# Mixer of a hybrid encoder: head sums by transpose and VectorE, and probabilities scaled before they are transposed, on one Trainium2 core

## Chip, core and metric

One core of a Trainium2 chip runs the whole program. The metric is the device time of one execution in microseconds (us); lower is better. Before the change it is 826.89 us, the median of 3 runs (826.85 to 827.06).

## What is computed

One layer of an encoder on 512 positions of width 1024, all in float32. Three stages follow each other:

```python
x = x + 0.5 * swiglu(rms_norm(x, ffn1_norm), ffn1_w_gate, ffn1_w_up, ffn1_w_down)
h = rms_norm(x, mix_norm)
u = h @ w_in                       # [ fourier 512 | q 8x64 | k 2x64 | v 2x64 ]
f_out = fourier_mixer(u[..., :o0], fnet_w, fnet_b)
a_out = gqa_attention(u[..., o0:o1], u[..., o1:o2], u[..., o2:], q_norm, k_norm)
x = x + jnp.concatenate([f_out, a_out], axis=-1) @ w_out
x = x + 0.5 * swiglu(rms_norm(x, ffn2_norm), ffn2_w_gate, ffn2_w_up, ffn2_w_down)
return rms_norm(x, final_norm)
```

The change touches the middle stage, and in it the attention:

```python
q = rms_norm(q.reshape(b, s, N_Q_HEADS, HEAD_DIM), q_norm)     # per head of 64
k = rms_norm(k.reshape(b, s, N_KV_HEADS, HEAD_DIM), k_norm)
q, k = apply_axial_rope(q, tables), apply_axial_rope(k, tables)
scores = jnp.einsum('bqhgd,bkhd->bhgqk', q_blk, k) * scale
p = jax.nn.softmax(scores, axis=-1)
return jnp.einsum('bhgqk,bkhd->bqhgd', p, v)
```

An `rms_norm` divides by the root of the mean square plus 1e-6. Since `q` and `k` come from `h`, whose own norm factor `r` (one number for each position) can be left out of the product and put in later, the kernel works on unnormed projections and corrects with `r` where it must.

## The kernel before

**Layout.** Activations lie transposed: the model width on the 128 partitions, the 512 positions along the free axis. A 128x512 float32 tile fills one of the eight PSUM banks. Every float32 factor is split into a high part in the format fp32r and the rest, so a product is two or three matmuls on TensorE (PE); ScalarE (ACT) rounds off the high part, VectorE (DVE) subtracts to get the rest (the helper `lows`, L127). Each weight chunk costs a 512 KB load on SP's queue (`raw_...`), a cast on ACT and a subtraction on DVE.

**Mixer.** The stage stands between the two FFNs. It is cut into named steps (`k.0`, `s001`, `e001` and so on), and a table `ORDER` lists all of them; the engines' queues are filled in exactly this order, each engine taking its own instructions from it. Nothing is reordered on the chip: an engine that reaches an instruction whose input isn't there waits, and everything listed behind it on that engine waits too. The eight banks are handed out in the order of the table as well: a step that takes a bank waits until the step that last reads the bank's former content is through.

The steps that matter here, with `t` the head pair 0 to 3, `b` the head of the pair, `c` a block of 128 queries and `kc` a block of 128 keys:

- `k.0` to `k.7`, `q0.0` and so on, `v.0` and so on: the projections, 3 matmuls of 512 columns each (L183). `n1.c`: the sum of squares of `x` over the partitions, 4 matmuls with a tile of ones as the moving operand, so 2 columns each (L241). `n1.m`, `n1.p`: mean, and the power -1/2 on GpSimd (POOL), which gives `r`. `n1.t`, `n1.b`: `r` transposed into a row over the free axis (4 PE transposes, L260) and copied out by ACT.
- `k.sq`, `q0.sq`: squares by ACT (L841). `.pq`: the sum of squares of each head, again 4 matmuls of 2 columns (`halves`, L889). `.s0`: three small DVE instructions that bring in `r` twice (L896, L898, L899); `.s1`: the power on POOL (L903); `.s2`: one more small DVE instruction (L907).
- `.sw`, `.rc`, `.rs`: the rotary embedding. `cos` loads its two tables on SP's queue. `.ah`, `.al`, `.bh`, `.bl`: the split of the rotated queries; `kw`, `kp`, `km`, `k0.0` and so on: the same for keys, after their factor was turned by 4 PE transposes (L946).
- `vt`, `vp`, `v0.h`, `v0.l`, `v1.h`, `v1.l`: values, scaled by the row of `r` on DVE, turned on PE and split.
- `s###`: two matmuls of 512 columns give the scores of 128 queries against all keys (L1150, L1151). `m###`: their maximum on DVE (L1156, L1157). `e###`: the exponential on ACT, with the sum `z` of each row as a by-product (L1164). `t###`: 4 PE transposes (L1176) turn a block so that keys lie on the partitions. `h###`, `l###`: the split by ACT (L1181) and DVE (L127). `v###`: two matmuls with the values (L1219).
- `z#.r`, `z#.w`, `z#.p`: 1/z by DVE (L1196), spread over 128 columns by POOL (L1201) and turned by 4 PE transposes (L1208); `o##.c`, `o##.a`: the two parts of the output added; `r#.m`: the multiplication by the turned 1/z on DVE (L1240); `r#.h`, `r#.l`: the split for the output projection.
- `f##.#`, `d##`, `c#.#`, `map#`: the Fourier group; `y#.#`: the output projection, 64 steps of 3 matmuls, of which `y#.0` to `y#.3` need the Fourier group alone.

Of the kernel before, what the change touches and what calls it, by code (L numbers as in the profile page):

```python
# [47 lines left out]
wk.r wq0.r wv.r wk.h wk.l wq0.h k.0 cos k.1 wv.h wq1.r wq0.l k.2 k.3 wv.l wq2.r k.4 k.5 k.6 k.7 k.sw k.rc k.rs  # L48
q0.0 f0.r q0.1 q0.2 q0.3 k.sq n1.c n1.m wq1.h n1.p wq1.l q0.4 q0.5 q0.6 q0.7 wq2.h q0.rc v.0 wq3.r q0.sw wq2.l
q1.0 k.pq k.s0 f2.r q0.rs q0.ah v.1 v.2 v.3 q0.sq q0.bh k.s1 k.s2 kw q0.al v.4 v.5 v.6 kp km n1.t n1.b v.7  # L50
wq3.h q0.bl pos vt wq3.l k1.2 q0.pq q1.1 q1.2 q0.s0 k1.0 k1.1 k1.3 vp q1.3 q1.4 q1.5 q1.6 q1.7 k0.0 k0.2 v0.h
k0.1 f1.r k0.3 s001 s000 q0.s1 q1.sw q0.s2 v0.l f0.h q1.sd s002 s010 m001 q1.sq q1.pq s003 q2.0 q2.1 q2.2 q2.3
m002 m010 q1.s0 e010 q2.4 q2.5 e001 q2.6 f0.l v1.h q2.7 m003 m000 e002 e003 s011 e000 t000 t001 h001 q1.rc
q1.rs v1.l q3.0 q2.sw f1.h f1.l m011 l001 h000 l000 q2.sd q2.sq t002 s012 m012 h002 fw.r l002 q1.ah q1.al
q2.rc q3.1 q3.2 q3.3 q3.4 q3.5 q3.6 q3.7 q1.bh q1.bl e012 s100 e011 s102 q2.rs q3.sw q3.rc s013 m013 t003 f2.h
q2.bh q1.s1 q1.s2 v000 v001 f00.0 f2.l v002 q3.sq m100 q2.pq e013 q3.sd m102 h003 l003 t010 q2.ah q2.al e100
t013 e102 s101 m101 e101 f00.1 q2.bl f00.u t011 h011 v003 q2.s0 s103 t012 q3.rs q3.bh l011 f02.0 m103 s110
q3.pq h010 l010 v010 v011 o00.c o00.a s201 h012 l012 s111 e103 q3.s0 t100 q3.bl h013 l013 q3.ah t102 h100 m110
v012 v013 o01.c f3.r f02.1 h102 l100 s112 q3.s1 m111 e111 o01.a t101 s113 z0.r z0.w l102 f01.0 h101 e110 m112
z0.p l101 q2.s1 v100 e112 v101 m113 e113 s203 s200 t103 r0.m r0.h f02.e h103 f02.h z1.r q3.s2 q2.s2 m200 z1.w  # L60
e200 l103 r0.l t110 h110 t112 q3.al f01.1 v102 m203 v103 o10.c m201 f01.u l110 o0.r s202 m202 h112 f03.0 o10.a
f03.1 f3.h v110 f03.e t113 e201 t111 f03.h s210 f3.l f03.l f10.0 f10.1 o1.r l112 s211 h111 l111 v111 h113 v112
e203 f10.u l113 s212 m210 m211 e202 t200 m212 t202 s300 f02.l e210 t201 h202 l202 e211 v113 m300 h200 f12.0
h201 l200 l201 f12.1 fw.h fw.l s213 m213 e212 s301 t203 o11.c z1.p v200 v201 v202 o11.a r1.m f12.e e213 t210
s303 h203 l203 e300 t211 h210 f11.0 h211 r1.h m301 l210 l211 s302 f12.h t212 v203 e301 m303 o20.c f13.0 m302
r1.l e302 f12.l s311 f11.1 h212 o20.a m311 z2.r t213 v210 f13.1 l212 s310 o0.h o0.l o3.r map0 o2.r h213 f11.u
l213 e303 t300 t302 f13.e o1.h m310 o1.l v211 v212 v213 t301 f13.h e310 f13.l d00 o21.c o21.a d10 map1 h302
z2.w l302 z2.p map0.h map0.l t303 h300 e311 s312 map1.h l300 v300 r2.m d20 h303 o2.h m312 d01 map1.l s313 d11
h301 l303 l301 v301 m313 d0.h d0.l v302 v303 c0.s e312 e313 t312 t311 o2.l d1.h d1.l o30.c c0.q c0.c d21 h312
o30.a o6.r t310 h310 l312 h311 c1.c c0.o c0.h d31 l310 t313 z3.r z3.w d2.h o4.r l311 c1.s c1.q v310 d30 d3.h  # L70
v311 h313 v312 c0.l y0.0 y1.0 d2.l c2.s r2.h c2.c c1.o l313 y2.0 v313 c1.h d3.l z3.p c2.q c3.c c2.o c2.h c1.l
c3.s c2.l y1.1 c3.q y0.1 o31.c y2.1 y2.2 c3.o c3.h c3.l y1.2 y1.3 y0.2 y0.3 y2.3 y0.4 r2.l y0.5 y0.6 o31.a
r3.m r3.h r3.l y0.7 o3.h o3.l y2.4 y2.5 y2.6 y1.4 y1.5 y1.6 y1.7 y1.x o4.h y3.0 o5.r y3.1 o4.l y3.2 y3.3 y3.4
y3.5 y2.7 o5.h y3.6 y3.7 o6.h y2.x o7.r y0.x o6.l y0.q y4.0 y4.1 y4.2 y4.3 y4.4 o5.l y4.5 y4.6 y4.7 y2.q y1.q
y4.x y3.x y5.0 y5.1 y5.2 y3.h o7.h y1.h o7.l y1.l y1.a y2.a y5.3 y6.0 y0.h y5.4 y0.l y3.q y3.a y4.h y5.5 y5.6
y5.7 y5.x y6.1 y6.2 y6.3 y6.4 y6.5 y6.6 y4.q y5.q y4.a y5.h y6.7 y6.x y6.h y7.0 y7.1 y7.2 y7.3 y6.q y4.l y2.h
y7.4 y7.5 y7.6 y7.7 y5.l y3.l y2.l y5.a y6.a y6.l y7.x y7.q y7.h y7.l y7.a
# [8 lines left out]
def encoder(ctx, tc, A, out):  # L86
# [660 lines left out]
    with tc.tile_pool(name="mix", bufs=1) as mp, tc.tile_pool(name="mixt", bufs=1) as mt:  # L747
# [9 lines left out]
        room(mp, 32)  # L757
# [122 lines left out]
        def heads_ops(name, t, factor):  # L880

            v = sc[:, :, 2 * t : 2 * t + 2]
            rx = n1.r.unsqueeze(2).to_broadcast([P, 4, 2])

            @op(f"{name}.pq")
            def _():
                banks[f"pq{name}"] = pq = bank_for(f"pq{name}")
                for c in range(4):
                    nc.tensor.matmul(  # L889
                        pq[:, 2 * c : 2 * c + 2], sqs[name][:, c * P : (c + 1) * P], halves, start=True, stop=True  # L890
                    )

            @op(f"{name}.s0")
            def _():
                pq = banks[f"pq{name}"][:, 0:8].rearrange("p (c t) -> p c t", t=2)
                nc.vector.tensor_tensor(out=v, in0=pq, in1=rx, op=ALU.mult)  # L896
                read(f"pq{name}")
                nc.vector.tensor_tensor(out=v, in0=v, in1=rx, op=ALU.mult)  # L898
                nc.vector.tensor_scalar(out=v, in0=v, scalar1=1.0 / HD, scalar2=EPS, op0=ALU.mult, op1=ALU.add)  # L899

            @op(f"{name}.s1")
            def _():
                nc.gpsimd.tensor_tensor(out=v, in0=v, in1=mhalf.rearrange("p (c t) -> p c t", t=2), op=ALU.pow)  # L903

            @op(f"{name}.s2")
            def _():
                nc.vector.scalar_tensor_tensor(out=v, in0=v, scalar=factor, in1=rx, op0=ALU.mult, op1=ALU.mult)  # L907
# [55 lines left out]
        @op("vt")  # L963
        def _():
            rots["v"] = tp.tile([P, S], F32, tag="g", name="vt")
            nc.vector.tensor_tensor(out=rots["v"], in0=banks["v"], in1=n1.rb, op=ALU.mult)
            read("v")

        @op("vp")
        def _():  # L970
            banks["vp"] = vp = bank_for("vp", 2)
# [3 lines left out]
        def value_ops(v):  # L975


            def own():
                return banks["vp"].rearrange("p (c v e) -> p c v e", c=4, v=2)[:, :, v, :]

            op(f"v{v}.h")(lambda: nc.scalar.copy(vst[:, v, :, 0, :], own()))

            @op(f"v{v}.l")
            def _():
                lows(vst[:, v, :, 1, :], own(), vst[:, v, :, 0, :])
                read("vp")

        for v in range(2):
            value_ops(v)

# [200 lines left out]
        def sum_ops(t):  # L1191


            @op(f"z{t}.r")
            def _():
                nc.vector.reciprocal(zs[t], zs[t])  # L1196

            @op(f"z{t}.w")
            def _():
# [367 lines left out]
```

## Time and profile before

| | us |
|---|---|
| median of 3 runs | 826.89 |
| the profiled execution | 827.06 |
| its span from first to last instruction | 824.8 |
| first FFN, from the start to | 331.06 |
| mixer, from there to | 489.87 |
| second FFN and final norm, from there to the end | 824.8 |

The stage borders are starts of matmuls on PE: the mixer's first one, and the first `gu` product of the second FFN. The profile counts an engine as busy from the start to the end of its instructions, and these overlap: on ACT and DVE an instruction often starts about 0.1 us before its forerunner's end, and on PE several matmuls are in flight at once. So two measures of an instruction's cost are needed, its duration and the distance to the next start. A wait is listed with the engine that waited, what it waited for, the total, the number of times and the longest.

### The profile page before, as it was taken

The page shows a single profiled execution, that of the slowest core. Times are in us where ns is not written, and L with a number is a line of the kernel's source. Part 1 is how long each engine was busy: PE and PEld are TensorE (multiplying, and loading weights), DVE is VectorE, ACT ScalarE, POOL GpSimd, SP SyncE. Part 2 cuts the span into 40 slices and gives each one's busy share as a digit, 9 for nine tenths or more (in the row PEclk, how much of TensorE's full clock was granted, in tenths as well). Part 3 has the DMA queues.
Part 4 walks back from the last instruction along what each step waited for, and adds up shares of the span by engine and source line. Part 5 has one row for each costly group of instructions (what it writes and reads, how often), then busy time and mean ns, then how long its engine had stood idle before and what let it go on. Part 6 is the DMA issues. An engine that isn't in the chain of part 4 may idle for free.

```text
span 824.8 us, 13679 instructions
## 1 busy us (share of the span) xinstructions
PE 816.9 (99%) x5406; PEld 750.4 (91%) x5406; DVE 639.2 (78%) x1005; ACT 464.6 (56%) x778; POOL 30.7 (4%) x34
## 2 busy tenths in 40 slices
PE   9999999999999999999999999999999999999997
PEld 7889999899989998888999888899988999899986
DVE  7998896489756947699998488998955896479574
ACT  7764664167524645677786357556632674256462
POOL 0110000000000000221100000100000000000001
PEclk9999999999999999999999999999999999999999
DMA  7664322323242213522020224453232332422222
GB/s 256 180 145 173 122 91 77 122 103 141 78 140 102 64 55 115 184 93 77 26 77 27 82 97 116 119 163 123 90 122 94 128 116 63 138 103 97 69 77 103
DMA packets 31168, 89.58 MB, mean 109 GB/s; under 512 B 3712, under 2 KB 8832, under 8 KB 31104
## 3 DMA queue, kind: packets, MB, share of 16 engines
q1 hardware_dynamic: 27776, 82.61, 29.2%
q0 software_dynamic: 2608, 5.12, 3.4%
q8 instruction: 42, 0.69, 0.3%
q10 hardware_dynamic: 720, 0.98, 0.3%
q14 instruction: 22, 0.18, 0.1%
HBM read 84.24 MB, written 2.10 MB: 105 GB/s over the span
## 4 chain that ended last, share of the span: by engine, by line
PE 92%; DVE 5%; issue 1%; ACT 0%; DMA 0%; POOLq 0%; POOL 0%; DVEq 0%; ACTq 0%
PE dn L183 25%; PE r L419 23%; PE q L419 12%; PE gu L183 8%; PE mix L183 7%; PE p L419 6%; PE gu L708 3%; PE mix L1219 1%; PE mix L1176 1%; DVE mx L1156 1%; PE mix L1073 1%; DVE pl L127 1%; PE mix L1015 1%; PE mix L1016 1%; PE mix L1014 1%
## 5 line engine op out<-in xcount | busy, mean ns | idle before, releaser
L419 PE MATMUL r<-rt,ring 128*128 128x256 f32 x1686 | 209.2, 276 | 0.0
L183 PE MATMUL dn<-at,ring 128*128 128x512 f32 x900 | 203.3, 381 | 0.5 <-DVE ring L127 0.4
L419 PEld LDWEIGHTS r<-rt,ring 128*128 128x128 f32 x1686 | 200.3, 188 | 0.8
L183 PEld LDWEIGHTS dn<-at,ring 128*128 128x128 f32 x900 | 168.0, 188 | 29.8 <-DVE ring L127 1.6
L419 PE MATMUL q<-rt,ring 128*128 128x256 f32 x840 | 106.6, 276 | 0.0
L127 DVE TENSOR_TENSOR ring<-s,ring 128x1024 fp32r<-128x1024 f32 x70 | 85.4, 1220 | 24.1 <-ACT ring L378 20.8
L419 PEld LDWEIGHTS q<-rt,ring 128*128 128x128 f32 x840 | 100.4, 188 | 0.0
L543 DVE SCALAR_TENSOR_TENSOR gx<-dn,gx 128x512 f32<-128x512 f32 x61 | 41.9, 688 | 67.6 <-PE dn L183 67.6
L378 ACT CAST ring<-s 128x1024 fp32r<-128x1024 f32 x70 | 73.5, 1050 | 28.0 <-PE p L419 13.7
L169 ACT CAST ring<-raw_dn 128x768 fp32r<-128x768 f32 (+3 forms) x58 | 45.2, 783 | 71.3 <-PE dn L183 62.1
L127 DVE TENSOR_TENSOR ring<-raw_dn,ring 128x768 fp32r<-128x768 f32 (+3 forms) x58 | 51.5, 891 | 5.6 <-PE r L419 4.4
L419 PE MATMUL p<-rt,ring 128*128 128x256 f32 x420 | 53.3, 276 | 0.0
L127 DVE TENSOR_TENSOR ring<-raw_g,ring 128x1024 fp32r<-128x1024 f32 x35 | 42.7, 1219 | 11.1 <-PE p L419 10.2
L419 PEld LDWEIGHTS p<-rt,ring 128*128 128x128 f32 x420 | 50.2, 188 | 0.0
L183 PE MATMUL gu<-ring 128*128 128x512 f32 x216 | 48.9, 381 | 0.0
L183 PEld LDWEIGHTS gu<-ring 128*128 128x128 f32 x216 | 40.4, 188 | 6.9
L378 ACT CAST ring<-raw_g 128x1024 fp32r<-128x1024 f32 x35 | 36.8, 1051 | 16.0 <-DMA raw_g<-in_wgu 8.8
L427 ACT COPY p<-r 128x256 f32<-128x256 f32 x35 | 12.9, 370 | 46.7 <-PE r L419 46.3
L451 ACT ACTIVATE g<-g 128x512 f32<-128x512 f32 x35 | 22.2, 633 | 23.4 <-DVE g L450 23.1
L387 ACT CAST ring<-raw_u 128x512 fp32r<-128x512 f32 x35 | 21.8, 624 | 16.6 <-PE q L419 16.0
L255 POOL TENSOR_TENSOR r<-ms,mhalf 128x4 f32<-128x4 f32 (+1 forms) x4 | 4.3, 1072 | 659.5 <-DVE ms L248 659.5
L464 DVE TENSOR_TENSOR u<-g,u 128x512 f32<-128x512 f32 x35 | 24.0, 685 | 6.1 <-ACT u L463 6.0
(271 smaller groups left out, 1323.1 us busy)
## 6 DMA issues: line engine op xcount, KB each, us to landing
raw_g<-in_wgu SPq DMA_DIRECT2D x35, 512.0 KB, 3.6
raw_u<-in_wgu SPq DMA_DIRECT2D x35, 512.0 KB, 4.3
raw_dn<-in_wd SPq DMA_DIRECT2D x40, 384.0 KB, 3.1
raw_gu<-in_wgu SPq DMA_DIRECT2D x12, 512.0 KB, 3.5
raw_o<-in_wo SPq DMA_DIRECT2D x8, 512.0 KB, 3.5
raw_dn<-in_wd SPq DMA_DIRECT2D x8, 448.0 KB, 3.4
raw_wq<-in_wins SPq DMA_DIRECT2D x4, 512.0 KB, 5.1
raw_f<-in_winf SPq DMA_DIRECT2D x4, 512.0 KB, 4.1
```

The source lines that it names most:

```text
L127: nc.vector.tensor_tensor(out=lo, in0=src, in1=asf(hi), op=ALU.subtract)
L169: nc.scalar.copy(hi[:, :n, :], raw[:, :n, :])
L183: nc.tensor.matmul(ps, a, b, start=first and b is mhi and a is whi, stop=last and a is wlo)
L378: nc.scalar.copy(hi, src)
L387: nc.scalar.copy(hi, src)
L419: nc.tensor.matmul(ps[:, t], a[:, ks], b[:, i, t], start=first and i == 0 and o == 0, stop=i == KH - 1 and o == 2, skip_group_check=not first,
L427: nc.scalar.copy(t, ps)
L451: nc.scalar.activation(b["g"], b["g"], AF.Silu)
L464: nc.vector.tensor_tensor(out=u, in0=b["g"], in1=u, op=ALU.mult)
L543: nc.vector.scalar_tensor_tensor(out=x[d][:, t], in0=ps[:, t], scalar=0.5, in1=x[d][:, t], op0=ALU.mult, op1=ALU.add)
L708: nc.tensor.matmul(turned(pss[c]), w[:, k % 2, c], turned(m[k]), start=k == 0 and m is hh and w is hi, stop=k == KD - 1 and w is lo,)
L1014: nc.tensor.matmul(ps, hh[k][:, cs], whi[:, a, :], start=k == 0, stop=False)
```

## The change

Four things, and a new `ORDER` table (633 steps before, 657 now).

1. The sums of squares (`n1.c` and the five `.pq`) no longer multiply with ones. The squares are transposed (4 PE transposes of 128 columns) and DVE adds along the free axis with one `tensor_reduce`. The small corrections with `r` are gone: instead of bringing `r` in twice, the eps is multiplied by the mean square of the position (`eps_ms`) and added to the sum. `.s2` is gone, and the factor that was in it is the key's `scalar1` in `kw`.
2. The row of `r` (`n1.t`, `n1.b`) is gone. Values are copied out by ACT, turned, and multiplied by `r` on DVE, now with positions on the partitions (`vs`); their split is one step each instead of two (`v.h`, `v.l`).
3. `z#.r`, `z#.w`, `z#.p` and `r#.m` are gone. For each pair of heads and query block DVE takes 1/z (`g##`, 128x2), and ACT multiplies each 128x512 block of probabilities by it in place (`n###`); the transposes `t###` now read these.
4. The order of everything around it.

```diff
-q0.0 f0.r q0.1 q0.2 q0.3 k.sq n1.c n1.m wq1.h n1.p wq1.l q0.4 q0.5 q0.6 q0.7 wq2.h q0.rc v.0 wq3.r q0.sw wq2.l
+wk.r wq2.r wq0.r wq1.r wk.h wk.l wv.r k.0 k.1 wq0.h k.2 wq0.l k.3 wq1.h k.4 k.5 k.6 k.7 n1.c k.sq q0.0 cos
...
-        room(mp, 32)
+        eps_ms = mp.tile([P, 8], F32, name="eps_ms")[:, :4]
...
-                    nc.tensor.matmul(
-                        pq[:, 2 * c : 2 * c + 2], sqs[name][:, c * P : (c + 1) * P], halves, start=True, stop=True
-                    )
+                    nc.tensor.transpose(pq[:, c * P : (c + 1) * P], sqs[name][:, c * P : (c + 1) * P], ident)
...
-                pq = banks[f"pq{name}"][:, 0:8].rearrange("p (c t) -> p c t", t=2)
-                nc.vector.tensor_tensor(out=v, in0=pq, in1=rx, op=ALU.mult)
+                pq = banks[f"pq{name}"].rearrange("p (c t e) -> p c t e", c=4, t=2)
+                nc.vector.tensor_reduce(out=v, in_=pq, axis=AX.X, op=ALU.add)
                 read(f"pq{name}")
-                nc.vector.tensor_tensor(out=v, in0=v, in1=rx, op=ALU.mult)
-                nc.vector.tensor_scalar(out=v, in0=v, scalar1=1.0 / HD, scalar2=EPS, op0=ALU.mult, op1=ALU.add)
+                nc.vector.tensor_tensor(out=v, in0=v, in1=er, op=ALU.add)
...
-            @op(f"{name}.s2")
-            def _():
-                nc.vector.scalar_tensor_tensor(out=v, in0=v, scalar=factor, in1=rx, op0=ALU.mult, op1=ALU.mult)
...
-                nc.vector.tensor_copy(kw, sc[:, :, 0:2].unsqueeze(3).to_broadcast([P, 4, 2, HD]))
+                nc.vector.tensor_scalar(
+                    out=kw, in0=sc[:, :, 0:2].unsqueeze(3).to_broadcast([P, 4, 2, HD]),
+                    scalar1=HD**0.5, scalar2=None, op0=ALU.mult,
+                )
...
-            nc.vector.tensor_tensor(out=rots["v"], in0=banks["v"], in1=n1.rb, op=ALU.mult)
+            nc.scalar.copy(rots["v"], banks["v"])
...
+        @op("vs")
+        def _():
+            nc.vector.tensor_tensor(
+                out=rots["v"].rearrange("p (c e) -> p c e", c=4),
+                in0=banks["vp"].rearrange("p (c e) -> p c e", c=4),
+                in1=n1.r.unsqueeze(2).to_broadcast([P, 4, P]), op=ALU.mult,
+            )
+            read("vp")
...
-        def sum_ops(t):
...
-                nc.vector.reciprocal(zs[t], zs[t])
...
-                nc.gpsimd.tensor_copy(zw, zs[t].unsqueeze(3).to_broadcast([P, 4, 2, HD]))
...
-                    nc.tensor.transpose(zps[t][:, c * P : (c + 1) * P], zs[t][:, c].rearrange("p a b -> p (a b)"), ident)
+        def sum_ops(t, c):
+            z = lambda b: zs[t][:, c, b : b + 1]
+
+            @op(f"g{t}{c}")
+            def _():
+                nc.vector.reciprocal(zs[t][:, c], zs[t][:, c])
+
+            for b in range(2):
+                op(f"n{t}{b}{c}")(lambda b=b: nc.scalar.activation(prob[t, b, c], prob[t, b, c], AF.Copy, scale=z(b)))
...
-                nc.vector.tensor_tensor(out=pair[t], in0=zps[t], in1=pair[t], op=ALU.mult)
...
-                n1.sum(banks["ss"], c, [n1.acc])
+                nc.tensor.transpose(ss[:, c * P : (c + 1) * P], n1.acc[:, c * P : (c + 1) * P], ident)
...
-            n1.mean(banks["ss"], 0, 4)
+            nc.vector.tensor_reduce(out=n1.ms, in_=banks["ss"].rearrange("p (c e) -> p c e", c=4), axis=AX.X, op=ALU.add)
             read("ss")
+            nc.vector.tensor_scalar(out=n1.ms, in0=n1.ms, scalar1=1.0 / D, scalar2=EPS, op0=ALU.mult, op1=ALU.add)
+            nc.vector.tensor_scalar(out=eps_ms, in0=n1.ms, scalar1=HD * EPS, scalar2=None, op0=ALU.mult)
```

**How the order moves instructions.** First place: PE at the start of the mixer, from the key projection (`mix0`) to the values or queries that follow. `mix` with a number is a PSUM bank. Before:

```order
L183 MATMUL mix0_3406<-ring_61 128x4x32x4 x24
L183 MATMUL mix1_3407<-ring_61 128x4x32x4 x12
L241 MATMUL mix2_3408<-ones_86,acc1_94 128x2 x4
L183 MATMUL mix1_3407<-ring_61 128x4x32x4 x12
L183 MATMUL mix3_3409<-ring_61,more_3401 128x4x32x4 x3
L183 MATMUL mix4_3410<-ring_61 128x4x32x4 x3
L889 MATMUL mix5_3411<-halves_111,sq_k_3482 128x2 x4
```

Now:

```order
L184 MATMUL mix0_3406<-ring_61 128x4x32x4 x24
L1286 MATMUL mix1_3407<-ident_106,acc1_94 128x128 x4
L184 MATMUL mix2_3408<-ring_61 128x4x32x4 x6
L890 MATMUL mix3_3409<-ident_106,sq_k_3460 128x128 x4
L184 MATMUL mix2_3408<-ring_61 128x4x32x4 x18
L184 MATMUL mix4_3410<-ring_61 128x4x32x4 x3
L943 MATMUL mix5_3411<-ident_106,kw_3414 128x128 x4
```

The sum over `x` follows the keys at once, the sum over the keys' squares 6 matmuls later instead of 30, and both are transposes of 128 columns where they were matmuls of 2.

Second place: ACT at the first probabilities, from the load of the exponential's table to the first casts of turned blocks (`ph`). `e` is a block of probabilities, `z0` their row sums. Before:

```order
L1164 ACT_TABLE_LOAD
L1164 ACTIVATE e010_3674,z0_3673<-mix7_3413,mx010_3667,sc_3405 128x512
L1164 ACTIVATE e001_3682,z0_3673<-mix5_3411,mx001_3641,sc_3405 128x512
L981 CAST near_3399<-mix2_3408 128x4x64
L1164 ACTIVATE e002_3698,z0_3673<-mix6_3412,mx002_3664,sc_3405 128x512
L1164 ACTIVATE e003_3700,z0_3673<-mix0_3406,mx003_3692,sc_3405 128x512
L1164 ACTIVATE e000_3704,z0_3673<-mix1_3407,mx000_3695,sc_3405 128x512
L1181 CAST ph001_3714<-mix5_3411 128x512
```

Now, the later part of the same piece:

```order
L1157 ACTIVATE e012_3687,z0_3637<-mix7_3413,mx012_3665,sc_3405 128x512
L912 CAST near_3399<-rot_q1_3603 64x512
L1192 ACTIVATE e002_3654<-e002_3654,z0_3637 128x512
L921 CAST near_3399<-rot_q1_3603 64x512
L1192 ACTIVATE e001_3643<-e001_3643,z0_3637 128x512
L1192 ACTIVATE e012_3687<-e012_3687,z0_3637 128x512
L1157 ACTIVATE e000_3732,z0_3637<-mix6_3412,mx000_3716,sc_3405 128x512
L1157 ACTIVATE e003_3734,z0_3637<-mix0_3406,mx003_3698,sc_3405 128x512
L963 COPY vt_3752<-mix1_3407 128x512
L1192 ACTIVATE e000_3732<-e000_3732,z0_3637 128x512
L1192 ACTIVATE e003_3734<-e003_3734,z0_3637 128x512
```

Before, the turned blocks came right after the five exponentials; now eight exponentials (of both heads, since `g##` takes a pair) and the in-place products (L1192) stand ahead of the first transposes, and the copy of the values (L963) has moved between them.

More of the change, by code (lines that the diff above doesn't have):

```diff
@@ L53 @@
[L53 to L57, printed above, removed]
@@ L1273, in output_ops @@
                 op(f"{name}.a")(lambda: nc.vector.tensor_tensor(out=n2.acc, in0=n2.acc, in1=sqs[name], op=ALU.add))
-        scale = HD**-0.5
         for c, n in enumerate(("k", "q0", "q1", "q2", "q3", "v")):
@@ L1278, in encoder @@
         rope_ops("k", qkg[:, 1:2])
-        heads_ops("k", 0, 1.0)
+        heads_ops("k", 0)
         key_ops()
@@ L1282, in encoder @@
             query_ops(t)
-            heads_ops(f"q{t}", t + 1, scale)
-            sum_ops(t)
+            heads_ops(f"q{t}", t + 1)
+            for c in range(4):
+                sum_ops(t, c)
             result_ops(t)
```

97 lines of the change are left out of this document (38 added, 59 removed).

## Prediction

> **What bounds the kernel now.** I read the page's first two parts first: is one engine full?
>
> ```profile
> span 824.8 us, 13679 instructions
> PE 816.9 (99%) x5406; PEld 750.4 (91%) x5406; DVE 639.2 (78%) x1005; ACT 464.6 (56%) x778; POOL 30.7 (4%) x34
> ```
>
> PE is busy for 99% of the span. A busy PE may still stretch its matmuls, so next I read busy time by stretches, for the mixer alone: its opening, the attention from the first score to the last weighted values, and what follows.
>
> ```profile
> core 0: us, PE busy (x) PEld busy (x) DVE busy (x) ACT busy (x) POOL busy (x), PEclk, DMA share, GB/s
> 331.06:356.11 25.05, 25.05 (x133) 21.76 (x132) 19.16 (x33) 17.39 (x25) 6.61 (x6) 1.00 0.61 205
> 356.11:448.41 92.30, 92.02 (x614) 83.55 (x613) 87.55 (x180) 71.38 (x145) 8.73 (x7) 1.00 0.16 52
> 448.41:489.87 41.46, 41.46 (x195) 35.50 (x193) 25.66 (x37) 17.31 (x26) 0.00 (x0) 1.00 0.22 77
> ```
>
> PE idles 0.28 us in the whole mixer, and its granted clock is 1.00 in each stretch. In the attention DVE is nearly full too (87.55 of 92.30) and ACT has 20.9 us free. The list of waits says how close DVE and ACT come to holding PE up:
>
> ```profile
> PEld mix L1150 <- ACT e L1164: 0.4, 1, 0.4
> PEld mix L1150 <- DVE pl L127: 0.4, 1, 0.4
> PEld mix L1176 <- ACT e L1164: 0.2, 1, 0.2
> ```
>
> Three short waits in 92 us. So PE's own work sets the end of the mixer, with two engines a step behind it, and every microsecond of PE work taken out counts in full as long as ACT and DVE stay ahead.
>
> **What leaves PE.** The chain of waits gives the price of each removed or added piece, as the time in which PE hands out its instructions:
>
> ```profile
> 331.06 7.92 PE mix L183 x36
> 338.98 0.79 PE mix L241 x8
> 343.86 0.79 PE mix L889 x8
> 349.17 0.44 PE mix L260 x4
> 393.38 0.44 PE mix L1208 x4
> ```
>
> Four matmuls of 2 columns appear as 8 records and take 0.79 us; four transposes of 128 columns take 0.44. The change replaces six such sums (`n1.c`, five `.pq`): out 6 x 0.79 = 4.74, in 6 x 0.44 = 2.64. It drops the row of `r` (L260) and four turns of 1/z (L1208): out 5 x 0.44 = 2.20. Together PE loses 4.74 + 2.20 - 2.64 = 4.30 us. All of it stands in the chain, so none was hidden.
>
> The one doubt is whether a transpose always costs 0.11.
>
> ```profile
> L1176 PE MATMUL mix<-ident,e 128*128 128x128 f32 x128 | 17.7, 272 | 0.0
> ```
>
> One lasts 272 ns from start to end, but neighbours overlap, so I take 0.11. If the new ones could not overlap, the 20 dropped and 24 added ones would go by 0.27, and PE would lose 4.74 - 4 x 0.27 = 3.65; I keep 3.65 as the lower end. A rule speaks against the change: the Trainium skill, "TensorE: Matmul & The Clock Gate", section "Part 4: PE-mode transpose", gives about 275 ns for a 128x128 transpose inside a kernel and says that transposes don't count as PE work for the full clock. The 272 ns agree with its figure; its clock effect isn't seen here, where 128 transposes ran in a mixer whose granted clock stayed 1.00. By the page's figure the sum would be the lower end, 3.65. With 4 transposes more than before in all, the clock rule gets no chance of its own.
>
> **What comes to ACT.** 32 multiplications of 128x512 by a number per partition. No row has exactly this; the nearest is the scaling by the gain (L209: from and to SBUF, 512 wide, scale per partition).
>
> ```profile
> L209 ACT ACTIVATE ring<-gx 128x512 fp32r<-128x512 f32 x9 | 6.3, 714 | 4.9 <-DVE gx L1262 4.9
> 332.77 0.72 ACT L209 ACTIVATE ring<-gx 128x512 fp32r<-128x512 f32 x1
> 333.40 0.62 ACT L219 ACTIVATE sq<-gx 128x512 f32<-128x512 f32 x1
> ```
>
> It lasts 0.714 but the next one starts 0.63 after it. So 32 cost ACT 20 us by starts, 22.8 by durations; I take 20, since ACT's queue in the attention is mostly back to back. Against the 20.9 us free that fills ACT to the brim, if the stretch stayed as it is. The new order stretches it: the first score now comes after 21.6 us of PE's work in the mixer instead of 24.8, and steps of the output projection move in before the last block, so that counted by these prices PE has 97.0 us of work between first score and last weighted values (90.3 before by the same prices, against 92.30 measured). Counted by starts in the same way, ACT has 88.6 us there and DVE 91.5.
>
> **DVE** comes out even.
>
> ```profile
> 356.90 0.68 DVE L1156 TENSOR_REDUCE mx<-mix 128x1 f32<-128x512 f32 x1
> 357.61 0.16 DVE L1157 TENSOR_TENSOR mx<-mx,sc 128x1 f32<-128x1 f32 x1
> 357.69 0.68 DVE L1156 TENSOR_REDUCE mx<-mix 128x1 f32<-128x512 f32 x1
> 395.31 0.19 DVE L1196 RECIPROCAL z<-z 128x8 f32<-128x8 f32 x1
> 395.42 0.19 DVE L907 SCALAR_TENSOR_TENSOR sc<-sc,r 128x8 f32<-128x8 f32 x2
> L1240 DVE TENSOR_TENSOR oo<-mix,oo 128x512 f32<-128x512 f32 x4 | 2.7, 687 | 0.1
> ```
>
> Six sums over 512 elements are new: by the maximum (L1156) 0.7 each, against four small instructions of 0.15 to 0.2 that go with each `.pq` and one that stays: +0.1 x 5, and +1.0 for `n1.m`. Sixteen reciprocals at 0.11 instead of four: +1.3. Four multiplications by the turned 1/z go: -2.7. The values' scaling only moves. Sum about 0. POOL loses four copies and gains nothing.
>
> **Where the new wait may come.** The transposes now need the scaled blocks, and a block can be scaled only after the exponentials of both heads and DVE's `g##`. I follow ACT from the second score of the new order (`s011`) to the first transposes (`t000`), with these starts:
>
> ```profile
> 359.44 1.28 ACT L1164 ACT_TABLE_LOAD   x1 [1.95 <-DVE sc L896]
> 360.74 0.78 ACT L1164 ACTIVATE e<-mix,mx,sc 128x512 f32<-128x512 f32 x1
> 361.50 0.77 ACT L1164 ACTIVATE e<-mix,mx,sc 128x512 f32<-128x512 f32 x1
> ...
> 366.58 0.69 ACT L849 ACTIVATE own_q<-mix,qkg 128x512 f32<-128x512 f32 x1
> 367.16 0.59 ACT L1181 CAST ph<-mix 128x512 fp32r<-128x512 f32 x1
> 367.63 0.62 ACT L841 ACTIVATE sq_q<-mix 128x512 f32<-128x512 f32 x1
> 368.12 0.61 ACT L1181 CAST ph<-mix 128x512 fp32r<-128x512 f32 x1
> 368.58 0.63 ACT L918 CAST near<-rot_q 64x512 fp32r<-64x512 f32 x1
> 369.24 0.62 ACT L927 CAST near<-rot_q 64x512 fp32r<-64x512 f32 x1
> 369.88 0.78 ACT L1164 ACTIVATE e<-mix,mx,sc 128x512 f32<-128x512 f32 x1
> ```
>
> After the score, about 1.0 for the maximum on DVE; table load 1.3; eight exponentials at 0.76 (360.74 to 361.50), 6.1; one `own` and one `sq`, 0.6 + 0.5; two query casts, 1.3; the values' copy, 0.5; five scalings at 0.63 and the last one's tail, 3.2. That is 14.5 us. PE has between the two 48 matmuls of 0.22 (36 take 7.92 in the chain), six pairs for scores at 0.44 and two groups of transposes at 0.44: 14.1 us.
>
> So PE waits some 0.4 us there, and everything listed behind `t000` with it. From there on ACT and DVE are each at 90 to 95% of PE, and the old order shows that this can be run with hardly a wait (DVE at 95%, three waits). But two engines are close now, and each `g##` on DVE waits for an exponential on ACT, with maxima queued behind it. I add 0.6 us for this, between 0 (both have room by the count above) and the rival's price below. New waits: 1.0; old waits gone: 0.28.
>
> **Sum.** The profiled execution took 827.06, of which 824.8 are the span; it lies 0.2 above the median. 827.06 - 4.30 - 0.28 + 1.0 = 823.5, and relative to the median **823.3 us**. With no wait at all it is 822.2, with transposes at their full length and waits of 1.9, 824.8: that is the forecast's own range.
>
> **Rivals.**
>
> *Faster, but the opening is late.* The load of `wv` now stands ahead of `cos` on SP's queue, and waits until DVE has read the buffer of `wq0`.
>
> ```profile
> 331.09 0.33 SPq L1300 DMA_DIRECT2D cos<-in_cos  x1
> 331.95 1.23 DVE L127 TENSOR_TENSOR ring<-raw_wq,ring 128x1024 fp32r<-128x1024 f32 x1 [0.17 <-ACT ring L812]
> raw_wv<-in_wins SPq DMA_DIRECT2D x1, 512.0 KB, 3.5
> cos<-in_cos SPq DMA_DIRECT2D x1, 256.0 KB, 2.7
> ```
>
> So `cos` goes out at 333.5 instead of 331.09 and lands between 336.2 and, if it shares the way with `wv`, 339.5; `k.rc` wants it at 338.0 (keys done at 336.3, four transposes, one reduce and two small ones). Up to 1.5 us late, with `k.rs`, `q0.rc`, the query casts and the first score behind it, which has 0.5 us of play by the same kind of count: 824.3.
>
> *About the same: the removed work was not what held the end.* If DVE's chain paces the attention, PE only trades work for waits: 826.9. For it: DVE's 95%. Against: DVE idles 4.7 us there while PE idles 0.28.
>
> *About the same, or slower: ACT and DVE hold each other up.* The sixteen `g##` stand in DVE's queue; when one waits for its exponential, the maxima behind it come late, hence the next exponentials, hence the next `g##`. DVE has 97.0 - 91.5 = 5.5 us of play; 3.6 of these were there before (90.3 - 86.7), and were needed, as the three waits show. So 1.9 us are free, and what sixteen waits take beyond that PE waits too. At 0.3 us each PE loses 2.9: 822.5 + 2.9 = 825.4. At one whole exponential each (0.77) it loses 10.4: **832.9, slower**. It decides from 0.5 us each on (8.0 - 1.9 = 6.1: 828.6). For it: ACT is near full, so an exponential is rarely early. Against: in the new table ACT's and DVE's work per 8 us of PE stays level, counted by these prices between 6.0 and 9.3 and between 6.6 and 10.5, with no stretch in which both pile up.
>
> **Chances.** Forecast 0.66, late opening 0.06, removed work not binding 0.05, mutual waits below 0.5 us each 0.12 (a quarter of it still faster), above 0.11. A measurement of this kernel tells a change of 0.2%, 1.65 us, from none. Faster by more: 0.66 + 0.06 + 0.03 = 0.75. Within: 0.09 + 0.05 = 0.14. Slower: 0.11. The range of 8 in 10 goes from 822.2 to 827.0: it leaves out the slow rival, a few hundredths of the mutual waits, and an even larger gain.
>
> **What would show it.** Right: PE's records fall by 48 (24 sums of 2 columns) and rise by 4 transposes, the mixer from first projection to first `gu` product takes 154.5 to 156 us instead of 158.8, the new scalings start 0.6 apart, ACT is busy above 85% of the attention, and PE idles at most 2 us there, the first time at `t000`. Wrong: scalings above 0.7 apart, or DVE waiting at the reciprocals for more than 0.3 us each (mutual waits); `k.rc` ended by the load of `cos` (opening); the mixer at 158 us or more with PE waiting on `pl` and `e` throughout.

## The result and the profile after

| | before | after |
|---|---|---|
| median, runs taken side by side, us | 826.97 (826.85 to 827.36, 4 runs) | 822.3 (821.47 to 822.44, 4 runs) |
| profiled execution, us | 827.06 | 822.25 |
| first FFN, to the mixer's first matmul | 330.90 | 331.46 |
| mixer, to the first `gu` product | 158.97 | 154.16 |
| the rest | 334.92 | 334.80 |

The ratio is 0.994 [0.9925, 0.9955]. On the forecast's scale that is 826.89 x 0.994 = 821.9 (820.7 to 823.2 by the interval): 1.4 below the forecast and 0.3 below the lower end of the range. The stages here begin where the first matmul starts; the chain of waits, which gave 331.06 and a mixer of 158.8, takes that matmul over a little later.

The page's first rows after the change:

```profile
span 820.4 us, 13609 instructions
PE 813.2 (99%) x5362; PEld 745.9 (91%) x5362; DVE 638.9 (78%) x1004; ACT 482.4 (59%) x809; POOL 28.1 (3%) x30
```

PE has 44 records fewer (48 of 2 columns out, 4 transposes in). Busy time by stretches, with the columns of the same view in the prediction: the mixer's opening, the attention, what follows.

```profile
331.46:353.36 21.90, 21.90 (x108) 18.50 (x107) 17.96 (x28) 16.61 (x24) 5.77 (x5) 1.00 0.52 180
353.36:451.94 98.58, 98.36 (x636) 88.61 (x635) 91.88 (x190) 91.59 (x181) 6.94 (x4) 1.00 0.18 60
451.94:485.62 33.68, 33.68 (x154) 28.72 (x153) 21.47 (x28) 15.82 (x23) 0.00 (x0) 1.00 0.24 79
```

PE fills each stretch, at a granted clock of 1.00. What changed in the attention is ACT's column: 91.59 of 98.58, where it had 71.38 of 92.30. ACT carries the new work and PE hardly sees it. The list of waits, first for PE and its weight loads, then a row of DVE's own:

```profile
PEld mix L1143 <- DVE near L128: 0.6, 1, 0.6
PE mix L1143 <- DVE near L128: 0.2, 1, 0.2
...
DVE z L1189 <- ACT e L1157: 0.9, 2, 0.7
```

One wait is left in the mixer, at a product of scores (L1143) and not at the transposes (L1169). The chain of waits over the stretch before it says what is late there; columns are start, us and the piece of work.

```profile
361.79 0.58 ACT own_q L850
362.37 0.77 ACT e L1157 x2
363.14 0.02 issue
363.16 0.17 DVE z L1189
363.32 0.60 DVE mx L1149
363.92 0.02 issue
363.95 0.16 DVE mx L1150
364.11 0.61 DVE mx L1149
...
365.74 0.70 DVE near L128
366.43 0.04 issue
366.48 0.49 PE mix L1143
```

Read it backwards. The score `s103` needs the rest of q1's split (`near`, step `q1.al`). DVE came to that late, because two maxima and a sum stand ahead of it, and ahead of these a reciprocal that waited 0.72 us for an exponential. The weights came 0.6 us late. What the stream of matmuls lost by it is read from the starts on PE:

```profile
365.42 0.84 PE L184 MATMUL mix<-ring 128*128 128x512 f32 x3
366.48 0.49 PE L1143 MATMUL mix<-ks,near 128*128 128x512 f32 x1 [0.22 <-DVE near L128]
366.80 0.39 PE L1144 MATMUL mix<-ks,near 128*128 128x512 f32 x1
```

Products of 512 columns start 0.22 apart here, so the third of the first row starts at 365.86. The next one follows 0.61 later and the one behind it 0.33 after that, where each distance is 0.22 otherwise: 0.50 in all. PE's idle time, 0.22, shows less than half of it.

The time from each PE instruction's start to the next one's, summed over the mixer by the width of the instruction, shows where the 4.81 us went (worked out from the trace's records; count and us):

| PE instructions in the mixer | before | after | |
|---|---|---|---|
| 2 columns | 48, 4.91 us | none | -4.91 |
| 128 columns | 156, 15.60 | 160, 15.31 | -0.29 |
| 512 columns | 478, 108.06 | 478, 108.38 | +0.32 |
| 256 and 258 columns | 256, 30.41 | 256, 30.48 | +0.07 |

A wait shows in two of these distances, the one up to the instruction that waits and the one behind it. At the new wait, in the 512-column row, they add up to the 0.50 above. At the two old ones, which stood behind groups of transposes, they are 0.41 and 0.33, where 0.03 and 0.31 are usual behind such a group: 0.41 us each, 0.81 together. So waits fell by 0.81 - 0.50 = 0.31, and the rest of the 4.81, 4.50 us, is PE's own work.

### The profile page after: what moved, and what is told of

It reads as the page before. It is cut to its first block, busy times and chain, and to the rows that moved or that the text cites. A ratio compares the mean times of both kernels' runs of the same rounds, so it can differ in the third digit from the quotient of the medians.

```text
span 820.4 us, 13609 instructions
## 1 busy us (share of the span) xinstructions
PE 813.2 (99%) x5362; PEld 745.9 (91%) x5362; DVE 638.9 (78%) x1004; ACT 482.4 (59%) x809; POOL 28.1 (3%) x30
## 4 chain that ended last, share of the span: by engine, by line
PE 93%; DVE 2%; ACT 1%; DMA 1%; issue 1%; POOL 0%; POOLq 0%; DVEq 0%; ACTq 0%
PE dn L184 25%; PE r L420 23%; PE q L420 12%; PE gu L184 7%; PE mix L184 6%; PE p L420 6%; PE gu L709 3%; PE mix L1203 2%; PE mix L1169 2%; PE mix L1007 1%; PE mix L1008 1%; PE mix L1009 1%; PE mix L1066 1%; PE mix L1143 1%; PE mix L1144 1%
## 5 line engine op out<-in xcount | busy, mean ns | idle before, releaser
L184 PE MATMUL mix<-near,ring 128*128 128x512 f32 x120 | 28.8, 381 | 0.0
```

What stands on the lines that cost most here:

```text
L184: nc.tensor.matmul(ps, a, b, start=first and b is mhi and a is whi, stop=last and a is wlo)
```

## The experiments

Eleven kernels, each compared with the kernel before on the same chip. "Mixer" is the time from the start of its first matmul to the start of the first `gu` product, in the profiled execution. It tells more than the median: over all the profiles the part before the mixer, whose code never changed, took between 330.7 and 331.8 us.

| run | median, us | ratio to before | mixer, us |
|---|---|---|---|
| the change | 822.3 | 0.994 [0.9925, 0.9955] | 154.16 |
| 20 transposes put back | 824.52 | 0.9967 [0.9953, 0.998] | 156.34 |
| sums by 2-column matmuls again | 824.34 | 0.9965 [0.9951, 0.9978] | 156.11 |
| scalings left out | 821.99 | 0.9935 [0.9922, 0.9949] | 154.13 |
| `q1.al` earlier | 822.04 | 0.9936 [0.9924, 0.9949] | 154.25 |
| 8 scalings doubled | 825.91 | 0.9985 [0.9975, 0.9995] | 158.45 |
| 16 scalings doubled | 832.21 | 1.006 [1.004, 1.008] | 163.95 |
| sums alone, old order | 829.13 | 1.0023 [1.0013, 1.0032] | 160.62 |
| scalings alone, old order | 847.17 | 1.0241 [1.0221, 1.0262] | 179.51 |
| `q1.al` and ACT's debts earlier | 822.35 | 0.9941 [0.9928, 0.9954] | 154.57 |
| n2's sum too | 822.02 | 0.9936 [0.9923, 0.9949] | 154.16 |
| the last two together | 823.17 | 0.9947 [0.9933, 0.9961] | 154.45 |

### Does PE's work set the mixer's length? Twenty transposes put back

Five groups of four transposes are issued twice, with the same result: the values' (`vp`) and the first block of each of the four head pairs.

```diff
-            for c in range(4):
+            for c in (0, 1, 2, 3) * 2:
                 nc.tensor.transpose(...)
...
-                for c in range(4):
+                for c in (0, 1, 2, 3) * (2 if (b, kc) == (0, 0) else 1):
```

> The changed kernel, with twenty PE transposes more (the four of vp and the first four of each head pair's t steps are issued twice into the same bank), as many as the change dropped for the row of r and for 1/z; nothing waits for them and nothing else differs. Theory (PE hands out instructions without a pause and each counts in full, 0.44 us per four): the mixer, from its first projection to the first gu product, takes 154.2 + 2.2 = 156.4 us, the kernel 822.3 + 2.2 = 824.5. Rival (ACT or DVE sets the pace of the attention, PE has room): mixer 154.2 to 154.8.

The mixer grew by 2.18 to 156.34, that is 0.109 per transpose, and the one wait stayed. A transpose in a group costs its place in PE's stream and nothing more, and no other engine's pace hides it.

### The sums alone put back

The six sums go back to matmuls with 2 columns, with `eps_ms` and everything else as in the change.

```diff
-                    nc.tensor.transpose(pq[:, c * P : (c + 1) * P], sqs[name][:, c * P : (c + 1) * P], ident)
+                    nc.tensor.matmul(
+                        pq[:, 2 * c : 2 * c + 2], sqs[name][:, c * P : (c + 1) * P], halves, start=True, stop=True
+                    )
...
-                nc.vector.tensor_reduce(out=v, in_=pq, axis=AX.X, op=ALU.add)
+                nc.vector.tensor_tensor(out=v, in0=pq, in1=er, op=ALU.add)
```

> The changed kernel with the six sums as matmuls of 2 columns again (one small DVE instruction in place of each 512 wide reduce, so DVE has about 4 us less). Theory (PE's issue): the removed sums cost 0.82 per four by the trace of before (48 records, 4.91 us) against 0.44, so the mixer takes 154.2 + 2.3 = 156.5 us. By the price that the prediction took (0.79 against 0.44): + 2.1. Rival (DVE sets the pace): the lighter DVE gives back what PE loses, mixer 154.2 or less; the wait before the score s103 (0.4 us, on the query rest q1.al) goes.

The mixer grew by 1.95. PE's list of waits is empty in this mixer: without the reduces DVE came to `q1.al` in time and the wait of 0.50 went, as the rival had said of it. 1.95 + 0.50 = 2.45 is the price of the swap, 0.41 for each of the six sums. That lies between the 0.38 of the expectation (0.82 against 0.44) and 0.47 by starts alike (0.82 up to the next matmul's start, against 0.35 for four transposes).

### Does ACT pace it? The scalings left out, and doubled

In the first of three kernels the 32 scalings are not issued, so 1/z is missing from the result. In the others 8 and 16 of them are followed by a second one, with a factor of one.

```diff
-                op(f"n{t}{b}{c}")(lambda b=b: nc.scalar.activation(prob[t, b, c], prob[t, b, c], AF.Copy, scale=z(b)))
+                op(f"n{t}{b}{c}")(lambda b=b: None)
```

```diff
+                def scaled(b=b):
+                    nc.scalar.activation(prob[t, b, c], prob[t, b, c], AF.Copy, scale=z(b))
+                    if b == 0 and c % 2 == 0:
+                        nc.scalar.activation(prob[t, b, c], prob[t, b, c], AF.Copy, scale=ones[:, 0:1])
```

(For 16, without `and c % 2 == 0`.)

> The changed kernel without the 32 scalings of the probabilities on ACT (1/z is left out of the result, the reciprocals stay): ACT has 20 us less in the attention. Theory (ACT keeps ahead of PE): only the one wait of 0.4 us can go, mixer 153.7 to 154.2 us. Rival (ACT, busy 91.6 of 98.6 us, paces part of the attention): mixer shorter by over 1 us.

> The changed kernel with 8 of the 32 scalings on ACT followed by one more multiplication of the same block by 1.0 (same form, 0.63 us each by their starts): 5.0 us more on ACT. ACT was busy 91.6 of the attention's 98.6 us, which leaves 7.0. Theory (room of some 7 us, spread over the attention): most of the 5.0 is hidden, mixer 154.2 to 156.5 us. Rival (ACT already sets the pace): all of it shows, mixer 159.2.

> The same with 16 more multiplications, 10.1 us on ACT, over the 7.0 us of room. Theory: at least 3.1 us show, and some more since the room is not where the work is: mixer 157.3 to 161 us. Rival (ACT already sets the pace): mixer 164.3. Third (ACT has far more room than its busy time says): mixer below 156.

Without the scalings the mixer takes 154.13 instead of 154.16. The stretch of the attention, in the columns used above:

```profile
353.40:452.00 98.60, 98.39 (x637) 88.67 (x636) 91.81 (x190) 73.43 (x149) 6.93 (x4) 1.00 0.19 60
```

ACT is busy for 73.43 instead of 91.59, and PE and DVE read the same: 18.2 us of busy ACT, 20 us by starts, cost nothing. In the other direction there was almost no room, at least where the work was put. Eight more scalings are 5.0 us by starts, and 4.29 of it shows, nearer to the rival's whole length than to the theory; sixteen are 10.1, and 9.8 shows. My count of room was refuted. With eight more, PE's weight loads wait at the transposes for scaled blocks (L1193 and L1195 are the first and second scaling) and behind them elsewhere:

```profile
PEld mix L1169 <- ACT e L1193: 1.6, 3, 1.1
PEld mix L1169 <- ACT e L1195: 1.0, 1, 1.0
PEld mix L1169 <- ACT fu L1019: 0.6, 1, 0.6
```

The room that ACT's idle time suggests isn't there when it is wanted. ACT's own list of waits in the attention of the change tells why:

```profile
ACT ph L1174 <- PE mix L1169: 2.2, 3, 1.6
ACT L1157 <- DVE mx L1150: 1.6, 1, 1.6
ACT fu L1019 <- PE mix L1009: 0.6, 1, 0.6
```

Of some 7 us without work, 1.6 pass before the first exponential and 2.2 at blocks that PE has yet to turn: there ACT waits for what others owe it. With eight scalings more these two still stand at 1.6 and 2.0, so the added work didn't go there. An added scaling also stands directly ahead of the transpose that reads it, so it can be late there while ACT idles elsewhere. How the 4.29 divides between lost room and this place wasn't told apart.

### Where does the remaining wait go? `q1.al` earlier

The order table alone is edited: `q1.al` moves ahead of two maxima and q1's sum.

```diff
-e013 v.2 m012 f1.r q2.sq q2.sw v.3 q1.rs f0.h q3.0 v.4 e012 s003 g01 g02 v.5 f3.r m003 q1.ah q1.pq q3.1 v.6
-q2.sd m000 q3.2 n002 v.7 q1.bh n001 q1.s0 n012 q1.al e000 e003 q1.s1 q1.bl f1.h s103 n1.p q3.3 g00 q3.4 g03
+e013 v.2 m012 f1.r q2.sq q2.sw v.3 q1.rs f0.h q3.0 v.4 e012 s003 g01 g02 v.5 f3.r q1.ah q1.al m003 q1.pq q3.1 v.6
+q2.sd m000 q3.2 n002 v.7 q1.bh n001 q1.s0 n012 e000 e003 q1.s1 q1.bl f1.h s103 n1.p q3.3 g00 q3.4 g03
```

> The changed kernel with one step moved in the order table: q1.al (the rest of the second query pair, on DVE) ahead of m003 and m000 and the sum q1.s0, so that it is ready before the score s103, where PE waited 0.4 us. Theory (that wait is what is left to gain, and the maxima that come 0.65 us later have room): mixer 153.8 us, the kernel 0.4 us faster than the changed one. Rival (two full engines: what is gained at s103 is lost at the next place, the exponentials of m003 and m000): mixer 154.2 or longer.

The wait at `s103` is gone, and PE now waits at the first transposes, in two pieces:

```profile
PEld mix L1169 <- ACT e L1192: 0.6, 2, 0.3
```

The 512-column instructions lost 0.54 us of their starts' distance and the 128-column ones gained 0.57; the mixer took 154.25. The two distances at `s103`, 0.61 and 0.33 in the change, are 0.24 and 0.24 here, which measures that wait a second time: 0.47. A part of the new wait is made by the edit itself, since the two maxima, and with them the last exponentials, now come later. ACT's four scalings for the first blocks show it, first in the change, then here:

```profile
368.11 2.57 ACT L1192 ACTIVATE e<-e,z 128x512 f32<-128x512 f32 x4
```

```profile
367.67 2.56 ACT L1192 ACTIVATE e<-e,z 128x512 f32<-128x512 f32 x4 [0.16 <-DVE z L1189]
```

They start 36.65 us after the mixer's first matmul in the change (at 331.46) and 36.94 here (at 330.73), 0.29 later. So an estimate of what PE is ahead of ACT at `t000` in the change itself, if nothing stopped it before, is 0.57 - 0.29, some 0.3 us. In the change the wait one place earlier covers it.

### Would both made early remove it? ACT's debts first

`q1.al` stands a little earlier than in the change, and the second half of q1's split (`q1.bh`, `q1.bl`) and the copy of the values (`vt`) leave the stretch in which ACT must scale the first blocks.

```diff
-q2.sd m000 q3.2 n002 v.7 q1.bh n001 q1.s0 n012 q1.al e000 e003 q1.s1 q1.bl f1.h s103 n1.p q3.3 g00 q3.4 g03
-q2.rc vt n000 q3.5 n003 vp m103 t000 f1.l vs t003 n011 f0.l n010 q3.6 e103 n013 q3.7 t001 h000 h001 t002
+q2.sd m000 q1.al q3.2 n002 v.7 n001 q1.s0 n012 e000 e003 q1.s1 f1.h s103 n1.p q3.3 g00 q3.4 g03 q1.bh
+q2.rc n000 q3.5 n003 vt m103 t000 f1.l t003 vp vs q1.bl n011 f0.l n010 q3.6 e103 n013 q3.7 t001 h000 h001 t002
```

> The changed kernel with one stretch of its written order set anew: between the second half of q2's rope and the four first transposes, q1's long multiply (q1.al) goes to VectorE ahead of q1's scale, and q1's shuffles, the casts vt and vp and the later half of q1's rope come after what ScalarE owes the first transposes. Theory: the 0.4 us that TensorE still waits in the mixer is one wait that moves between two places (the product s103 that needs q1, and the first transposes, that need ScalarE's first scalings); with both made early it goes, and the mixer takes 153.8 us instead of 154.2, the kernel 0.4 us less than the change. Rival: the wait moves to a third place (kp and the v casts, or the second group), mixer 154.2 or more.

The mixer took 154.57, 0.4 more than the change: the rival's result. The waits sit in a third place, mostly behind the rest of a turned block (`pl`) that DVE now reaches later:

```profile
PEld mix L1143 <- DVE pl L128: 0.5, 1, 0.5
PEld mix L1007 <- DVE pl L128: 0.3, 1, 0.3
PEld mix L1169 <- ACT e L1192: 0.2, 1, 0.2
```

Three orders, and about 0.5 us or more of waiting in each: around 366 to 375 us DVE and ACT together seem to be about that much behind PE, and moving steps among themselves moved the place. With six reduces less on DVE (the sums put back) there was no wait on the list. That no order avoids it isn't shown.

### The last 2-column sum: n2's, in the opening of ffn2

The same swap where the row of 1/rms is still needed; the row is asked for one step later.

```diff
+            if self.n == 2:
+                for c in range(4):
+                    nc.tensor.transpose(ps[:, c * P : (c + 1) * P], self.acc[:, c * P : (c + 1) * P], ident)
+                nc.vector.tensor_reduce(out=self.ms, in_=ps.rearrange("p (c e) -> p c e", c=4), axis=AX.X, op=ALU.add)
...
-gate(1, {3: row})
+gate(1, {4: row})
```

> The changed kernel with the last sum of squares by a matmul with two columns, n2's in the opening of ffn2, made by four transposes and one VectorE reduce as well. Theory: the price per sum is TensorE's issue time alone, four two-column matmuls 0.82 us against four transposes 0.44, so what follows the mixer takes about 0.35 us less and the mixer stays at 154.2. Rival: the row of 1/rms, which is still needed here, comes later by the reduce and the wait for it takes the gain back: 0.0, or a loss of a few tenths.

> The two edits before this together, on the changed kernel. Theory: they lie in different stages and add, 0.75 us less than the change (mixer 153.8, the rest after it 0.35 less). Rival: one or both bring nothing, 0.0 to 0.4 less.

The swap itself gave what a sum is worth: four transposes hand PE on after 0.35, where eight records had taken 0.82, and the down projection began 37.90 us after the first `gu` product instead of 38.38. But the part behind the mixer took 335.16, against 334.80 in the change. In the kernel with both edits it took 335.14. PE's timeline of the first of the two, and ACT's, show where it went:

```profile
671.50 1.65 PE L427 MATMUL q<-rt,ring 128*128 128x256 f32 x12 [0.47 <-ACT p L435]
```

```profile
667.38 0.84 ACT L170 CAST ring<-raw_dn 128x768 fp32r<-128x768 f32 x1 [1.38 <-DMA raw_dn<-in_wd]
```

In the profile of the change the same cast on ACT waited for the same load, for less, and PE didn't wait behind it:

```profile
667.73 0.84 ACT L170 CAST ring<-raw_dn 128x768 fp32r<-128x768 f32 x1 [0.76 <-DMA raw_dn<-in_wd]
```

PE came earlier and met a load that took longer. It too went out earlier, at 662.50 against 663.47 in the change, but landed at 667.35 against 667.70: 4.86 us from issue to landing instead of 4.24. Both kernels with the edit show this wait, the others don't; why the load takes longer wasn't tried. One profile of each is thin ground besides: in the eight kernels that have the change's code behind the mixer, this part took between 334.66 and 335.50, the longest with a wait of 1.2 for DVE at a down projection, 0.4 in the change. The medians, 822.02 and 823.17 with five runs each, can't tell such small gains from none, and no version was found that beats the change by more than its own runs scatter.

### What does the new order do? Each part alone in the old one

First the sums by transposes and `eps_ms`, with the row of `r`, the turned 1/z and the old table (only the empty `.s2` taken out of it). Then, in a kernel of its own, 1/z by ACT: for each head the reciprocal and four scalings stand right behind the head's fourth exponential, and often its first transposes follow at once; `z#.r`, `z#.w`, `z#.p` and `r#.m` are gone.

```diff
-m002 m010 q1.s0 e010 q2.4 q2.5 e001 q2.6 f0.l v1.h q2.7 m003 m000 e002 e003 s011 e000 t000 t001 h001 q1.rc
+m002 m010 q1.s0 e010 q2.4 q2.5 e001 q2.6 f0.l v1.h q2.7 m003 m000 e002 e003 s011 e000 g00 n000 n001 n002 n003 t000 t001 h001 q1.rc
```

> The kernel before with the first part of the change alone (the six sums by transposes and DVE, without the small corrections by r), in the order of before. PE loses 6 x (0.82 - 0.44) = 2.3 us, DVE gains about 1 us of work. Theory (PE's issue, whatever the order): mixer 158.97 - 2.3 = 156.7 us, kernel 824.6. Rival (the new order is needed, since DVE at 95% cannot take more in the old one): mixer 157.5 to 159.5.

> The kernel before with the third part alone (reciprocal per head of a pair on DVE, 32 scalings on ACT right after the fourth exponential of each head and ahead of its first transposes; the turned 1/z and its product are gone), otherwise in the order of before. PE loses 4 x 0.44 = 1.8 us, DVE 2.7. Theory (the new order is what makes the scalings free): PE waits at the first transposes of most of the eight heads for a reciprocal and four scalings, 1 to 2.5 us each, mixer 158.97 - 1.8 + 8 to 20 = 165 to 177 us. Rival (ACT's 20.9 us of room suffices in any order): mixer 157 to 159.

Neither gains. The sums alone made the mixer 1.65 longer instead of 2.3 shorter, above the range of the rival too (157.5 to 159.5). PE's work went down by the 24 two-column matmuls, but PE now waits in many places, mostly for DVE, which has the new reduces in its queue:

```profile
PEld mix L1146 <- DVE pl L127: 1.1, 1, 1.1
PEld mix L1215 <- DVE pl L127: 1.0, 2, 0.7
PEld mix L1172 <- ACT e L1160: 0.9, 1, 0.9
PEld mix L942 <- DVE kw L933: 0.8, 1, 0.8
PEld mix L183 <- DVE ring L127: 0.7, 1, 0.7
```

The scalings alone made it 20.5 longer, about the 20 us that all 32 take on ACT: the theory's loss, 2.5 above its upper end of 177. PE waits for nearly every one (L1147 are the transposes, L1170 the scalings):

```profile
PEld mix L1147 <- ACT e L1170: 17.0, 30, 1.6
```

The table of the change gives the blocks time between the scaling and the transpose. My placement gives none, so 20.5 is the price of this insertion and not of every one in the old order.

## Why the prediction was right or wrong

**The kind was right, two sizes were off.** The forecast took 3.6 us off the median, and 4.67 went. In the mixer the prediction's terms give -4.30 - 0.28 + 1.0 = -3.58, measured -4.81. Of the 1.23 between them 0.53 is the old waits, 0.50 the new waits and 0.20 PE's work. (The sum without any wait is 822.3 by the prediction's own terms, not 822.2.) The steps:

- *PE's own work sets the mixer.* Held. Twenty transposes put back cost 2.18 of mixer, to the transpose. The rival that the removed work wasn't binding (826.9) is refuted by this run and by the sums put back.
- *Six sums and five groups of transposes leave PE: 4.30.* Measured 4.50, a little mis-sized. The chain's prices aren't taken alike. Up to the next matmul's start four 2-column matmuls take 0.82 and four transposes 0.35, and the product behind either takes 0.09 longer than usual, so 6 x 0.47 + 5 x 0.44, about 5.0, leave. Some 0.5 of it comes back in small pieces: 512-column products among their like start 0.2221 apart after the change and 0.2209 before, some 400 times; why wasn't tried. The transposes put back ran at 0.109 each, so the lower end of 3.65, with every transpose at its full length, was 0.85 off. The Trainium skill, "TensorE: Matmul & The Clock Gate", section "Part 4: PE-mode transpose", gives about that full length, 275 ns, for bf16 in one kernel, and the group rows here agree (L1169 and L890, 272 ns, float32), but as a price in a stream the measurement decides: 0.109.
- *Old waits gone: 0.28.* This step failed: measured 0.81. The prediction had the list of waits, with 0.4 and 0.4, beside it and took PE's idle time instead. A matmul in flight counts as busy while the next one waits for its weights. The starts of the profile before show it, in the rows of PE's weight loads and matmuls around the second wait:

```profile
390.31 0.58 PEld L1176 LDWEIGHTS mix<-ident,e 128*128 128x128 f32 x4
391.27 0.19 PEld L1150 LDWEIGHTS mix<-ks,near 128*128 128x128 f32 x1 [0.38 <-ACT e L1164]
```

```profile
390.54 0.60 PE L1176 MATMUL mix<-ident,e 128*128 128x128 f32 x4
391.27 0.50 PE L1150 MATMUL mix<-ks,near 128*128 128x512 f32 x1
```

  Four transposes from 390.54 hand on after 0.35 elsewhere, here at 390.89; the next matmul starts at 391.27, 0.38 later, and the one behind it is 0.03 late as well: 0.41. PE counts as idle for 0.14 of it alone, since the last transpose runs to about 391.13, and twice 0.14 is the prediction's 0.28. The other old wait, at 378.62, reads the same.
- *New waits: 1.0.* This step failed as well: measured 0.50. The first of the forecast's two parts, 0.4 at `t000`, comes near this in size, but partly by luck: the wait stands 3 us earlier, at `s103`, and is for DVE and not for ACT. One at `t000` appeared when that place was cleared, and by the estimate above some 0.3 of it was hidden in the change. The second part, 0.6 for the rest of the attention, wasn't there: after 366.48 us PE's list shows no wait in the mixer. An allowance added to a count that already balanced was too much.
- *Scalings 0.63 apart on ACT, 20 us, off the path.* Held: the median distance of starts is 0.62, for 0.728 each.

```profile
L1192 ACT ACTIVATE e<-e,z 128x512 f32<-128x512 f32 x32 | 22.4, 728 | 0.1
L1189 DVE RECIPROCAL z<-z 128x2 f32<-128x2 f32 x16 | 2.4, 158 | 1.0 <-ACT e L1157 0.9
```

  Leaving them out changed nothing. But the reading that ACT at 88.6 of 97.0 had room was wrong: 5.0 us more cost 4.29.
- *ACT and DVE hold each other up.* Its mechanism is in the trace: the reciprocal's wait of 0.72 stands in the chain that made `q1.al` late. Its size isn't: 0.9 us in 2 of 16 reciprocals, far from 0.3 to 0.77 in each. It is one link of the wait that cost PE 0.50.
- *The opening.* Refuted. `k.rc` needs `cos`, which went out at 334.19, 2.73 us after the mixer's first matmul (the prediction's 333.5 is 2.6 after it), and landed 4.0 us later, inside the range that I worked out. A row of SP's queue and one of DVE:

```profile
334.19 0.38 SPq L1279 DMA_DIRECT2D cos<-in_cos  x1
```

```profile
338.68 0.75 DVE L872 SCALAR_TENSOR_TENSOR rot_k<-mix,qkg,cos 128x512 f32<-128x512 f32 x1 [0.19 <-ACT ring L813]
```

  The load was there at 338.2. DVE's instruction before ended at 338.49 (338.32 and 0.17 long), so DVE came to `k.rc` after the load, and its row puts the last 0.19 down to ACT.
- *The order.* The prediction looked for places where the new order would wait, and didn't ask what the parts would cost without it. In the old order, at the places tried, the sums lost 1.65 and the scalings 20.5, where they were worth 2.3 and 1.8 by PE's work; so the gain needs the order as much as the edits. Which moves in it matter wasn't tried one by one.

With the measured sizes in the forecast's own sum, 826.89 - 4.50 - 0.81 + 0.50 = 822.1.

## What to carry to other kernels

Where one engine runs without gaps, price an edit by the distance of its instructions' starts, waits included, and not by idle time or durations; then ask of every place where another engine hands over what is late there, and count each wait once. Before giving an engine with free time new work, look at what that free time waits for: here 32 scalings cost nothing, and a quarter more of them, put right behind the first, cost nearly their full length. A change in the work and the order around it are one edit: each of these two parts, put into the old order, made the kernel slower.

## What the runs showed of the hardware

TensorE starts at about half rate, and how long it stays there differs from profile to profile. Matmuls of 512 columns start 0.427 us apart at first and 0.220 later; the step came at 3.72 us in the profile before and at 6.36 in the profile after, in code that is the same. The rows of PE from 5 to 7 us, before and after:

```profile
5.03 2.27 PE L708 MATMUL gu<-ring 128*128 128x512 f32 x9 [0.71 <-ACT ring L694]
```

```profile
4.92 2.29 PE L709 MATMUL gu<-ring 128*128 128x512 f32 x6
```

Nine products begin in the one, six in the other, since more of those after the change are slow: counted from the start, it has nine distances of 0.427 where the profile before has six. Three times 0.21 is about the 0.57 by which its mixer starts later, which hides a part of the gain in the profiled execution. The granted clock in the profile reads 1.00 in both stretches and doesn't show it. So the prediction's 1.00 for the mixer doesn't settle by itself that transposes leave the clock alone here; the 512-column starts 0.22 apart in the mixer do. The Trainium skill, "TensorE: Matmul & The Clock Gate", section "Part 1: The HAM clock gate (the "warmup" mystery)", has a free-running window of about 3.4 us after which the clock doubles, so that the number of slow matmuls differs between runs; the two steps, 2.6 us apart and so within one such window, agree.

Four matmuls with 2 columns held TensorE over twice as long as four transposes with 128 (0.82 and 0.35 up to the next matmul's start): the profile lists each of them as two records, most of them 0.11 us apart. And a sum over 512 elements on VectorE took as long as an elementwise instruction of that width (0.68 and 0.69), so each swapped sum costs VectorE one full-width instruction.
